# Low parts of the weights on GpSimd in the S5 stage, four small memsets per batch on VectorE, and projection units shared out anew

## The chip, the cores and the metric

One core of a Trainium2 chip runs the whole block in one launch. The metric is the device time of that launch in microseconds (us), as the median of several runs; lower is better. In the profile the engines are PE (TensorE matmuls), PEld (its weight loads), DVE (VectorE), ACT (ScalarE), POOL (GpSimd) and SP (SyncE, which here issues nearly all DMAs). Each engine works through its own list in order, and so does each DMA queue.

## The reference

A decoder block on x (1024 tokens x 1024 channels, float32). The input is normalised and projected by one wide matrix; the pieces of the projection feed an mLSTM branch, an S5 branch and two gates:

```python
xn = rmsnorm(h, norm_pre_g[l])
proj = xn @ w_in[l]
u_a, z_a, o_a, i_a, f_a, u_b, z_b, g_pre = jnp.split(proj, split_points, axis=-1)
y_a = mlstm_branch(...) @ w_a_out[l]
y_b = s5_branch(u_b, z_b, ...) @ w_b_out[l]
g = jax.nn.sigmoid(g_pre)
merged = g[..., :D_MODEL] * y_a + g[..., D_MODEL:] * y_b
h = h + rmsnorm(merged @ w_o[l], norm_post_g[l])
```

The S5 branch is a diagonal complex recurrence over the sequence with 32 groups of 64 states, then a gelu, a product with `w_glu` under a sigmoid (the gate product) and silu(z_b).

## The kernel before, in words

**Matmuls in three passes.** Every large product is made in a rounded 32-bit type. An operand `a` is split in a high part (`a` rounded, made on ACT) and a low part (`a` minus the high part), and a product is three matmuls: high by high, high by low, low by high. For the activations these are the tiles `xh` and `xl`, for the weights `wh` and `wl`. `split_w` (L130) makes a weight's two halves of 128x1024: ACT copies `wh` from the raw tile `wr` (L140), and the subtraction for `wl` (L142) runs on DVE, except for a few later weights whose second half goes to POOL. `wr`, `wh` and `wl` have two buffers each.

**How weights flow.** A planned list (`plan`) fixes the order of the weights. `take` hands out the weight that is due and at once splits the next one (`pump`). After a split, `fetch` asks for the weight after that: an SP DMA of `wr`, which has to wait until ACT and the engine of `wl` have read the old `wr`. SP works in order, so stores that are queued behind this DMA wait with it.

**Units.** The projections for the gates (`g`, seven weights with four units each, after an eighth that is done at the start) and for `z_b` (`zb`, two weights with four units each) are cut in units of 24 matmuls on 512 columns. They lie in a first-in first-out list, `fillers`, and are called units 0 to 35 here: 0 to 27 are `g`, 28 to 35 are `zb`. `take` of a new weight comes with units 0, 4, 8, and so on. `fill(n)` runs the next n. A unit writes one of three PSUM banks (`pp`); ACT makes a tanh of it into one of three `tg` buffers, for `zb` units DVE also multiplies with the bank (L309), and SP stores `tg` to DRAM (`t_d`, `zb_d`).

**The S5 stage.** Its 32 groups are worked in four batches b of eight. Per batch:

- `s5_pre` and `s5_phase` (DVE): tables `w_r`, `w_i`, `v_r`, `v_n`, and the phases `ec_r`, `ec_i` and decays `rho`, in 12 and 42 products and sums and a copy.
- `s5_w`, `s5_k` (PE): transposes of the tables and a small kernel; ACT copies them out, POOL clears `m0` (L647), DVE adds to `kt_` (L644), and DMAs fill `m0` by way of DRAM.
- `s5_x` (PE, 32 small matmuls, L661), and then its chain on DVE: four products with PSUM, two sums, two scans (L675, L676), four products and four sums that end in `ss_`.
- `s5_y` (PE, L701 with `m0` and L702 with `ss_`), gelu on ACT (L705), eight stores to `yg_d`.

POOL sets single columns of `ec_r`, `ec_i`, `rho` and `ss_` by small memsets (L604, L605, L615, L678).

The order around them is written out by hand. Ten units lie ahead of the batches. In each batch stand `s5_w`, `s5_k`, two units, `s5_x`, then on DVE `s5_pre` and `s5_phase` of the next batch, three units (two in the last batch), `s5_y`, one unit. One unit follows the batches. Then the four `yg` tiles are loaded (L738), split into `ygh` (ACT, L742) and `ygl` (DVE, L743), two units follow, and with all 36 used up the gate product (`glu_unit`, on `ygh`, `ygl`) begins.

Of the kernel before, what the change touches and what calls it, by code (L numbers as in the profile page):

```python
# [36 lines left out]
def hybrid_block(ctx, tc, x, norm_pre_g, w_in, conv_w, conv_b, w_q, w_k, w_v, b_i, b_f, head_g,  # L37
# [4 lines left out]
    V, A, PE, PL, SY = nc.vector, nc.scalar, nc.tensor, nc.gpsimd, nc.sync  # L42
# [11 lines left out]
    def mbank():  # L54
        return ps.tile([P, 512], F32, tag="pm", bufs=5, name="pm")
# [54 lines left out]
    def dma_w(parts, kt, ncol):  # L110
# [16 lines left out]
            raws.append((k0, n, raw, 0, ncol))  # L127
        return raws

    def split_w(kt, ncol, raws, between=None, pl=False):  # L130
        wh = wp.tile([P, kt, ncol], F32R, tag="wh", name="wh")
        wl = wp.tile([P, kt, ncol], F32R, tag="wl", name="wl")
        if "M" in cur and kt == 2 and ncol == 512:
            pm = cur.pop("M")
            A.activation(wh[:, :, 0:256], pm, AF.Copy)
            tt(wl[:, :, 0:256], pm, wh[:, :, 0:256].bitcast(F32), ALU.subtract)
            raws = [(0, 2, raws[1], 256, 256)]
        for i, (k0, n, raw, c0, w) in enumerate(raws):
            hi = wh[:, k0:k0 + n, c0:c0 + w]
            A.activation(hi, raw, AF.Copy)  # L140
            eng = PL if (between or pl) and i else V
            eng.tensor_tensor(wl[:, k0:k0 + n, c0:c0 + w], raw, hi.bitcast(F32), op=ALU.subtract)  # L142
            if between and i == 0:
                between()
        return wh, wl
# [14 lines left out]
    def pump(between=None, pl=False):  # L160
        if not ready:
            fetch()
            if raw_q:
                key, kt, ncol, raws = raw_q.popleft()
                ready.append((key, split_w(kt, ncol, raws, between, pl)))
        pending.append(fetch)
# [35 lines left out]
    def run(u):  # L202
        tick()
        pre, body = u
        if pre:
            pre()
        for i in range(min(look[0], len(fillers))):
            if fillers[i][0]:
                fillers[i][0]()
                fillers[i] = (None,) + fillers[i][1:]  # L210
        while early:
            early.pop(0)()
        new = len(stage2)
        body()
        fresh = stage2[new:]
        del stage2[new:]
        step2()
        stage2.extend(fresh)

    def fill(n=1):  # L220
        for _ in range(n):
            if fillers:
                run(fillers.popleft())

    def unit(body, pre=None):
        return (pre, body)
# [137 lines left out]
    def b4k(name, shape, bufs=1, tag=None):  # L364
        return sp.tile(list(shape), F32, tag=tag or name, bufs=bufs, name=name)

    def ub_unit(b, hf):
        if b % 2 == 0 and hf == 0:
            cur["ub"] = take(("ub", b // 2))
        if hf == 0:  # L370
            uc[b] = b4k("uc", (P, TS, P), 4, "u0")
        o = bank()
        proj_cm(o, cur["ub"], (b % 2) * P, xh, xl, HS[hf])
        A.copy(uc[b][:, :, 64 * hf:64 * hf + 64], o.rearrange("p (c t) -> p t c", t=TS))
        if hf:
            ut[b] = b4k("ut", (P, 8, P), 4)
            store(u_d[b], uc[b].rearrange("p t c -> p (t c)"))
            defer(lambda: store(ut[b], u_d[b].rearrange("(g m) (j c) -> (m j) g c", m=NG, j=TS)))
# [12 lines left out]
    def ubstep():  # L391
        if ub_steps:
            b, hf = ub_steps.popleft()
            run(unit(lambda: ub_unit(b, hf)))
        else:
            fill()
# [21 lines left out]
                             src[0, 16 * gh:16 * gh + 16].rearrange("(a b) n p -> b a n p", b=2)[b])  # L418
    for _ in range(4):
        ubstep()  # L420
    pt = mbank()
    for j in range(3):
        PE.transpose(pt[:, j * GP:(j + 1) * GP], prm[:, j, :], ident[:GP, :GP])
# [14 lines left out]
    def tt(o, a, b, op):  # L438
        V.tensor_tensor(o, a, b, op=op)  # L439

    def mul(o, a, b):
        tt(o, a, b, ALU.mult)
# [71 lines left out]
    def cmul(o_r, o_i, xr, xi, yr, yi, t=None, t2=None):  # L514
        n = 1
        for s in o_r.shape[1:]:
            n *= s
        if t is None:
            t = cm_t[0][:, :n]
            if len(o_r.shape) == 3:  # L520
                t = t.rearrange("p (a b) -> p a b", a=o_r.shape[1])
        mul(o_r, xr, yr)
        mul(t, xi, yi)
        tt(o_r, o_r, t, ALU.subtract)
        t2 = t if t2 is None else t2
        mul(o_i, xr, yi)
        mul(t2, xi, yr)
        tt(o_i, o_i, t2, ALU.add)

    def bc(a, shape):  # L530
        return a.to_broadcast(shape)
# [68 lines left out]
    def s5_phase(b):  # L600
        gs = slice(4 * b, 4 * b + 4)

        ec_r, ec_i = b4k("ec_r", (P, 4, P)), b4k("ec_i", (P, 4, P))
        PL.memset(ec_r[:, :, 0:1], 1.0)  # L604
        PL.memset(ec_i[:, :, 0:1], 0.0)  # L605
        te = b4k("te", (P, 4, 64))
        for k in range(7):
            n = 1 << k
            yr = bc(ph[3 + k][0][:, gs].unsqueeze(2), [P, 4, n])
            yi = bc(ph[3 + k][1][:, gs].unsqueeze(2), [P, 4, n])  # L610
            cmul(ec_r[:, :, n:2 * n], ec_i[:, :, n:2 * n], ec_r[:, :, 0:n], ec_i[:, :, 0:n], yr, yi,
                 te[:, :, :n])
        rho = b4k("rho", (P, 4, P))
        V.tensor_copy(rho, bc(rho8[:, gs].unsqueeze(2), [P, 4, P]))
        PL.memset(rho[:, :, 0:1], 0.0)  # L615
        st[b].update(ec=(ec_r, ec_i), rho=rho)

    def s5_w(b):
        q = st[b]
        wt = b4k("wt", (P, 2, 4, P))  # L620
        for ri, w in enumerate(q["w"]):
            pt = mbank()
            for g in range(4):
                PE.transpose(pt[:, g * P:(g + 1) * P], w[:, g].rearrange("p m s -> p (m s)"), ident)
            A.copy(wt[:, ri].rearrange("p g c -> p (g c)"), pt)
        q["wt"] = wt
# [28 lines left out]
    def s5_x(b):  # L655
        q = st[b]
        xr, xi = mbank(), mbank()
        for g in range(4):
            for b2 in range(2):
                for ri, o in enumerate((xr, xi)):  # L660
                    PE.matmul(o[NS * b2:NS * (b2 + 1), g * P:(g + 1) * P],  # L661
                              q["wt"][:, ri, g, NS * b2:NS * (b2 + 1)], ut[b][:, 2 * g + b2, :],
                              start=True, stop=True)
        ec_r, ec_i = q["ec"]
        er, ei = ec_r.rearrange(fl), ec_i.rearrange(fl)
        zr, zi, zt = b4k("zr", (P, 512)), b4k("zi", (P, 512)), b4k("zt", (P, 512))
        zt2 = b4k("zt2", (P, 512))
        mul(zr, xr, er)
        mul(zt, xi, ei)
        mul(zi, xi, er)  # L670
        mul(zt2, xr, ei)
        tt(zr, zr, zt, ALU.add)
        tt(zi, zi, zt2, ALU.subtract)
        rf = q["rho"].rearrange(fl)
        V.tensor_tensor_scan(zr, rf, zr, 0.0, op0=ALU.mult, op1=ALU.add)  # L675
        V.tensor_tensor_scan(zi, rf, zi, 0.0, op0=ALU.mult, op1=ALU.add)  # L676
        ss_ = b4k("ss_", (P, 2, 4, P))
        PL.memset(ss_[:, :, :, 0:1], 0.0)  # L678
        g4 = lambda a: a.rearrange("p (g c) -> p g c", c=P)[:, :, 0:P - 1]
        zrs, zis, t_a, t_b = g4(zr), g4(zi), g4(zt), g4(zt2)  # L680
        ers, eis = ec_r[:, :, 0:P - 1], ec_i[:, :, 0:P - 1]
        mul(t_a, zis, eis)
        mul(t_b, zis, ers)
        mul(zis, zrs, eis)
        mul(zrs, zrs, ers)
        for b2 in range(2):
            rows = slice(NS * b2, NS * (b2 + 1))
            tt(ss_[0:NS, b2, :, 1:], zrs[rows], t_a[rows], ALU.subtract)
            tt(ss_[NS:P, b2, :, 1:], zis[rows], t_b[rows], ALU.add)
        q["s"] = ss_  # L690
# [22 lines left out]
    while ub_steps:  # L713
        ubstep()
    fill(3)
    s5_phase(0)
    for b in range(4):
        s5_w(b)
        s5_k(b)
        fill(2)  # L720
        s5_x(b)
        if b < 3:
            s5_pre(b + 1)
            s5_phase(b + 1)
        fill(3 if b < 3 else 2)
        s5_y(b)
        fill(1)
    s5.close()
# [23 lines left out]
    def load_aux(key, src):  # L752
        t = gq.tile([P, 512], F32, tag="aux", bufs=6, name="aux")
        SY.dma_start(t, src)
        aux[key] = t
# [31 lines left out]
    for i in range(2):  # L787
        for hf in range(2):
            for m in range(4):
                ct = 4 * i + m  # L790
                fillers.append(unit(lambda i=i, m=m, hf=hf: yb_unit(i, m, hf),
                                    lambda ct=ct, hf=hf: load_aux((1, ct, hf), t2_d[ct * P:(ct + 1) * P, HS[hf]])))
    look[0] = 3
    while fillers:
        fill()
    look[0] = 1
# [660 lines left out]
```

## Time and profile before

| what | value |
|---|---|
| median of 3 runs | 1003.8 us (1002.75 to 1004.91) |
| the profiled execution: its own time, its span | 1006.37 us, 1004.3 us |
| PE busy | 976.7 us, 97% of the span |
| DVE, ACT, POOL busy | 61%, 35%, 15% of the span |
| share of PE in the chain that ended last | 83% |
| mean granted TensorE clock | 0.993 |
| S5 batches in the trace | about 146 to 306 us from the start |
| gate product starts | 328.4 us |

A line of the profile gives the kernel's line, engine, operation and the tiles written and read; behind the bar stand busy time, mean duration in ns, and idle time with what ended it. A line of the timeline gives the start in us from the span's start and the duration. In the view of waits the three numbers are the total in us, how often, and the longest.

### The profile page before, as it was taken

How to read it: one execution, taken by the hardware profiler on the slowest of the kernel's cores; microseconds unless marked ns; L12 is line 12 of the kernel's file. 1: busy time of each engine (PE TensorE's matmuls, PEld its weight loads, DVE VectorE, ACT ScalarE, POOL GpSimd, SP SyncE). 2: the span in 40 equal slices, each digit the busy share in tenths (PEclk: the TensorE clock that was granted, in tenths of full speed). 3: DMA queues.
4: the chain of work that ended last, by engine and by line, in shares of the span. 5: the costliest groups of instructions: out<-in, count | busy, mean ns of one | idle time of the engine just before them, and what ended most of it. 6: DMA issues, size and time to landing. Idle time of an engine off the chain costs nothing.

```text
span 1004.3 us, 15220 instructions
## 1 busy us (share of the span) xinstructions
PE 976.7 (97%) x5617; PEld 840.9 (84%) x5617; DVE 615.5 (61%) x1400; ACT 351.1 (35%) x696; POOL 154.6 (15%) x210
## 2 busy tenths in 40 slices
PE   7999999999999999999999999999999999999997
PEld 6888888788778788978988899889987888779997
DVE  4426496686952854254677477747774888675226
ACT  7322131233032531223544355435543452223311
POOL 4001000000000000012112232223221311343001
PEclk8999999999999999999999999999999999999999
DMA  7344221333056447314433354336436796783504
GB/s 253 94 153 157 90 95 36 93 111 109 17 177 187 170 156 253 107 42 126 138 121 131 95 174 131 135 86 184 132 121 215 248 318 202 271 301 118 189 1 168
DMA packets 115449, 148.31 MB, mean 148 GB/s; under 512 B 19080, under 2 KB 71472, under 8 KB 115376
## 3 DMA queue, kind: packets, MB, share of 16 engines
q1 hardware_dynamic: 115376, 147.35, 45.7%
q8 instruction: 44, 0.72, 0.3%
q14 instruction: 29, 0.24, 0.1%
HBM read 100.88 MB, written 46.43 MB: 147 GB/s over the span
## 4 chain that ended last, share of the span: by engine, by line
PE 83%; DVE 10%; DMA 3%; issue 2%; ACT 1%; SPq 0%; POOL 0%; DVEq 0%; POOLq 0%; ACTq 0%
PE pp L180 22%; PE pp L182 22%; PE pp L181 22%; PE pm L182 4%; PE pm L180 4%; PE pm L181 3%; DVE wl L142 1%; PE pm L1084 1%; DMA wr<-in_w_in_dram 1%; DVE zt L439 1%; PE pm L1007 1%; DMA xt<-in_x_dram 1%; DMA ft<-t_d 1%; PE pm L661 1%; DVE ec_r L439 1%
## 5 line engine op out<-in xcount | busy, mean ns | idle before, releaser
L180 PE MATMUL pp<-xh,wh 128*128 128x512 f32 x768 | 307.6, 401 | 3.2 <-DVE xl L276 2.4
L182 PE MATMUL pp<-xh,wl 128*128 128x512 f32 x768 | 305.0, 397 | 4.4 <-DVE wl L142 4.4
L181 PE MATMUL pp<-xl,wh 128*128 128x512 f32 x768 | 304.7, 397 | 0.0
L182 PEld LDWEIGHTS pp<-xh,wl 128*128 128x128 f32 x768 | 145.0, 189 | 41.0 <-DVE wl L142 6.2
L180 PEld LDWEIGHTS pp<-xh,wh 128*128 128x128 f32 x768 | 145.0, 189 | 39.3 <-DVE xl L276 2.7
L181 PEld LDWEIGHTS pp<-xl,wh 128*128 128x128 f32 x768 | 145.1, 189 | 32.7
L142 DVE TENSOR_TENSOR wl<-wr,wh 128x1024 fp32r<-128x1024 f32 (+2 forms) x71 | 83.4, 1211 | 46.3 <-ACT wh L140 41.7
L140 ACT ACTIVATE wh<-wr 128x1024 fp32r<-128x1024 f32 (+2 forms) x76 | 73.2, 1008 | 40.8 <-PE pm L181 30.7
L182 PE MATMUL pp<-wh,ml 128*128 128x256 f32 x256 | 72.8, 284 | 0.5 <-POOL ml L1363 0.5
L180 PE MATMUL pp<-wh,mh 128*128 128x256 f32 x256 | 72.9, 285 | 0.0
L180 PE MATMUL pp<-wh,xh 128*128 128x256 f32 (+1 forms) x256 | 72.0, 281 | 0.0
L181 PE MATMUL pp<-wl,mh 128*128 128x256 f32 x256 | 71.9, 281 | 0.0
L288 ACT ACTIVATE tg<-pp 128x512 f32<-128x512 f32 x32 | 19.1, 599 | 151.1 <-PE pp L182 75.2
L181 PE MATMUL pp<-wl,xh 128*128 128x256 f32 (+1 forms) x256 | 71.8, 280 | 0.0
L182 PE MATMUL pp<-wh,xl 128*128 128x256 f32 (+1 forms) x256 | 71.8, 280 | 0.0
L182 PEld LDWEIGHTS pp<-wh,ml 128*128 128x128 f32 x256 | 48.1, 188 | 0.7 <-POOL ml L1363 0.7
L181 PEld LDWEIGHTS pp<-wl,mh 128*128 128x128 f32 x256 | 48.6, 190 | 0.1
L180 PEld LDWEIGHTS pp<-wh,mh 128*128 128x128 f32 x256 | 48.4, 189 | 0.2 <-ACT mh L1362 0.2
L181 PEld LDWEIGHTS pp<-wl,xh 128*128 128x128 f32 x256 | 48.2, 188 | 0.2
L180 PEld LDWEIGHTS pp<-wh,xh 128*128 128x128 f32 x256 | 48.1, 188 | 0.2
L182 PEld LDWEIGHTS pp<-wh,xl 128*128 128x128 f32 x256 | 48.0, 187 | 0.0
L981 POOL TENSOR_TENSOR hll<-t2k,hlh 128x512 fp32r<-128x512 f32 x16 | 20.8, 1297 | 166.2 <-ACT hlh L980 89.4
(395 smaller groups left out, 1731.5 us busy)
## 6 DMA issues: line engine op xcount, KB each, us to landing
wr<-in_w_in_dram SPq DMA_DIRECT2D x48, 512.0 KB
t_d<-tg SPq DMA_DIRECT2D x32, 256.0 KB
xt<-in_x_dram SPq DMA_DIRECT2D x8, 512.0 KB
aux<-t_d SPq DMA_DIRECT2D x16, 256.0 KB
gb_d<-aux SPq DMA_DIRECT2D x16, 256.0 KB
so_d<-sow SPq DMA_DIRECT2D x32, 128.0 KB
sz_d<-t2k SPq DMA_DIRECT2D x16, 256.0 KB
cs_d<-t2k SPq DMA_DIRECT2D x16, 256.0 KB
```

The costliest lines, as they stand in the source:

```text
L140: A.activation(hi, raw, AF.Copy)
L142: eng.tensor_tensor(wl[:, k0:k0 + n, c0:c0 + w], raw, hi.bitcast(F32), op=ALU.subtract)
L180: PE.matmul(o, lh, rh, start=first, stop=False)
L181: PE.matmul(o, lh, rl, start=False, stop=False)
L182: PE.matmul(o, ll, rh, start=False, stop=last)
L288: A.activation(t, o, AF.Tanh, scale=0.5)
L439: V.tensor_tensor(o, a, b, op=op)
L661: PE.matmul(o[NS * b2:NS * (b2 + 1), g * P:(g + 1) * P], q["wt"][:, ri, g, NS * b2:NS * (b2 + 1)], ut[b][:, 2 * g + b2, :], start=True, st ...
L981: PL.tensor_tensor(lo, acc, hi.bitcast(F32), op=ALU.subtract)
L1007: PE.matmul(pm[:, 256 * k:256 * k + 256], wt[:, e, 256 + P * k:256 + P * k + P], wt[:, e, 0:256], start=e == 0, stop=e == 1)
L1084: PE.matmul(sc[:, :P], k_[:, m, sl], q_[:, m, sl], start=m == 0, stop=m == 1)
```

## The change

The flag `lo_pool` is set after the fourth of the eight `ub` units (the projections that feed S5) and taken back when the gate product's units are started. While it is set, `split_w` gives both low halves of a weight to POOL. This holds for ten weights: the seven `g` of the units, the two `zb` and the gate product's own.

```diff
+    lo_pool = [False]
...
-            eng = PL if (between or pl) and i else V
+            eng = PL if lo_pool[0] or (between or pl) and i else V
...
     for _ in range(4):
         ubstep()
+    lo_pool[0] = True
...
-        PL.memset(ec_r[:, :, 0:1], 1.0)
-        PL.memset(ec_i[:, :, 0:1], 0.0)
+        V.memset(ec_r[:, :, 0:1], 1.0)
+        V.memset(ec_i[:, :, 0:1], 0.0)
...
-        PL.memset(rho[:, :, 0:1], 0.0)
+        V.memset(rho[:, :, 0:1], 0.0)
...
-        PL.memset(ss_[:, :, :, 0:1], 0.0)
+        V.memset(ss_[:, :, :, 0:1], 0.0)
...
     for b in range(4):
         s5_w(b)
         s5_k(b)
-        fill(2)
+        fill(1 if b < 3 else 2)
         s5_x(b)
         if b < 3:
             s5_pre(b + 1)
             s5_phase(b + 1)
-        fill(3 if b < 3 else 2)
+        fill(3)
         s5_y(b)
         fill(1)
...
     look[0] = 3
+    lo_pool[0] = False
     while fillers:
         fill()
```

The units keep their order. The first three batches have five units each now and the last has six, so units 10 to 30 lie in the batches (10 to 32 before), and six units, 30 to 35, stand between the last `s5_y` and the gate product, where four stood.

What moves on POOL: the rows from the clearing of the `bd` tables (ahead of the batches) to the causal masks of the next stage. Before:

```order
L550 MEMSET bd_i 128x512
L604 MEMSET ec_r 128x4
L605 MEMSET ec_i 128x4
L615 MEMSET rho 128x4
L647 MEMSET m_1435 128x1024
L678 MEMSET ss__1532 128x8
```

And now, in the same place and on through all four batches:

```order
L553 MEMSET bd_i 128x512
L144 TENSOR_TENSOR wl<-wr,wh 128x1024 x4
L650 MEMSET m_1435 128x1024
L144 TENSOR_TENSOR wl<-wr,wh 128x1024 x2
L650 MEMSET m_1763 128x1024
L144 TENSOR_TENSOR wl<-wr,wh 128x1024 x2
L650 MEMSET m_2091 128x1024
L144 TENSOR_TENSOR wl<-wr,wh 128x1024 x4
L650 MEMSET m_2425 128x1024
L144 TENSOR_TENSOR wl<-wr,wh 128x1024 x4
L819 MEMSET tri 128x128
```

The small memsets are gone from POOL, and between two clearings of `m0` (`m_...`) stand two to four halves of low parts.

On DVE, the end of the last batch's tables and the start of its chain behind `s5_x`. Before:

```order
L614 COPY rho<-rex 128x512
L142 TENSOR_TENSOR wl<-wr,wh 128x1024 x2
L644 SCALAR_TENSOR_TENSOR kt__2505<-eye_1213,par,kt__2505 128x16
L142 TENSOR_TENSOR wl<-wr,wh 128x1024 x2
L309 SCALAR_TENSOR_TENSOR tg<-tg,pp 128x512 x2
L439 TENSOR_TENSOR zr<-pm,ec_r 128x512
```

And now:

```order
L617 COPY rho<-rex 128x512
L618 MEMSET rho 128x4
L647 SCALAR_TENSOR_TENSOR kt__2417<-eye_1213,par,kt__2417 128x16
L442 TENSOR_TENSOR zr<-pm,ec_r 128x512
L442 TENSOR_TENSOR zt<-pm,ec_i 128x512
```

Four halves of low parts and the products of two `zb` units have left the place ahead of `zr`, the first product of the chain.

On ACT, from the last gelu to the gate product's first tanh (`par` is its bias). Before:

```order
L705 ACTIVATE yg<-pm 128x4x128 x2
L140 ACTIVATE wh<-wr 128x1024 x2
L308 ACTIVATE tg<-pp 128x512 x2
L742 ACTIVATE ygh_2794<-yg_2792 128x1024
L742 ACTIVATE ygh_2800<-yg_2798 128x1024
L742 ACTIVATE ygh_2806<-yg_2804 128x1024
L742 ACTIVATE ygh_2812<-yg_2810 128x1024
L308 ACTIVATE tg<-pp 128x512 x2
L140 ACTIVATE wh<-wr 128x1024 x2
L764 ACTIVATE tg<-pp,par 128x512
```

And now:

```order
L708 ACTIVATE yg<-pm 128x4x128 x2
L310 ACTIVATE tg<-pp 128x512 x2
L745 ACTIVATE ygh_2726<-yg_2724 128x1024
L745 ACTIVATE ygh_2732<-yg_2730 128x1024
L745 ACTIVATE ygh_2738<-yg_2736 128x1024
L745 ACTIVATE ygh_2744<-yg_2742 128x1024
L142 ACTIVATE wh<-wr 128x1024 x2
L310 ACTIVATE tg<-pp 128x512 x4
L142 ACTIVATE wh<-wr 128x1024 x2
L767 ACTIVATE tg<-pp,par 128x512
```

Four tanh instead of two now follow the four `ygh`, and the split of the gate product's own weight has moved from ahead of them to behind them.

## The prediction

> **What bounds the kernel now.** First the page's busy times, then PE's waits in the stretch from 60 to 340 us, which holds all that the change touches.
>
> ```profile
> PE 976.7 (97%) x5617; PEld 840.9 (84%) x5617; DVE 615.5 (61%) x1400; ACT 351.1 (35%) x696; POOL 154.6 (15%) x210
> ```
>
> ```profile
> PE pp L182 <- DVE wl L142: 2.2, 2, 1.1
> PE pm L702 <- DVE ss__2622 L439: 2.0, 2, 1.3
> PE pp L181 <- DVE ygl L743: 1.9, 2, 1.0
> ```
>
> PE is the bound, and the change leaves its matmuls as they are. It can only win back time that PE loses, and in this stretch PE loses it in three places, each waiting for DVE: twice for the low part of a weight, twice for `ss_` in the last `s5_y`, twice for `ygl` at the gate product. What each place costs is read better from PE's timeline, from start to start of equal work, because it also holds slow matmuls.
>
> ```profile
> 187.40 0.27 PE L624 MATMUL pm<-ident,w_r 128*128 128x128 f32 x1
> ...
> 201.70 2.02 PE L661 MATMUL pm<-ut,wt 128*64 128x128 f32 x32
> ...
> 220.55 0.38 PE L701 MATMUL pm<-ut,m 128*128 128x128 f32 x2
> ...
> 224.04 0.48 PE L180 MATMUL pp<-xh,wh 128*128 128x512 f32 x1
> ...
> 229.74 0.38 PE L624 MATMUL pm<-ident,w_r 128*128 128x128 f32 x2
> ...
> 242.69 2.02 PE L661 MATMUL pm<-ut,wt 128*64 128x128 f32 x32
> ...
> 298.29 0.38 PE L701 MATMUL pm<-ut,m 128*128 128x128 f32 x2
> 299.99 0.46 PE L702 MATMUL pm<-ss__2622,vs 128*128 128x128 f32 x2 [1.31 <-DVE ss__2622 L439]
> ...
> 301.40 0.72 PE L702 MATMUL pm<-ss__2622,vs 128*128 128x128 f32 x2 [0.73 <-DVE ss__2622 L439]
> ...
> 305.92 0.48 PE L180 MATMUL pp<-xh,wh 128*128 128x512 f32 x1
> ...
> 328.41 0.40 PE L180 MATMUL pp<-ygh,wh 128*128 128x512 f32 x1
> ...
> 333.88 0.50 PE L180 MATMUL pp<-ygh,wh 128*128 128x512 f32 x1
> ...
> 336.77 0.39 PE L180 MATMUL pp<-ygh,wh 128*128 128x512 f32 x1
> ```
>
> - From `s5_w` to `s5_x` the batch at 229.74 takes 12.95 us, the batch at 187.40, with a wait for `wl`, 14.30: 1.35 lost. The other wait for `wl` is as long, so 2.7 in all.
> - `s5_y` takes 224.04 - 220.55 = 3.49, the last one 305.92 - 298.29 = 7.63: 4.1 lost. Only 2.0 of this is waiting.
> - The gate product's first two units of 12 matmuls take 5.47 and 2.89: 2.6 lost.
>
> Together 9.4 us. The 2.1 in the last `s5_y` that aren't waiting are clock:
>
> ```profile
> 300.00:306.00 6.00, 5.27 (x31) 5.11 (x31) 2.52 (x4) 0.24 (x1) 0.00 (x0) 0.72 0.24 90
> ```
>
> The granted clock is 0.72 over 6 us, so 1.7 us are lost by a slow clock right behind two gaps of 1.31 and 0.73. I take it that it goes with the gaps. [...]
>
> **The change part by part.**
>
> *Low parts off DVE.* Why DVE is late, from its timeline around a batch, the queues' waits and the groups:
>
> ```profile
> 161.38 0.69 DVE L439 TENSOR_TENSOR zr<-pm,ec_r 128x512 f32<-128x512 f32 x1 [9.30 <-PE pm L661]
> ...
> 172.94 0.69 DVE L439 TENSOR_TENSOR w_r<-bb_r,pv_r 128x512 f32<-128x512 f32 x1
> ...
> 181.07 0.16 DVE L439 TENSOR_TENSOR ec_r<-ec_r,ph_r 128x4 f32<-128x4 f32 x1
> ...
> 189.50 2.35 DVE L142 TENSOR_TENSOR wl<-wr,wh 128x1024 fp32r<-128x1024 f32 x2
> ...
> 289.74 0.68 DVE L439 TENSOR_TENSOR zr<-pm,ec_r 128x512 f32<-128x512 f32 x1
> ```
>
> ```profile
> SPq L124 <- DVE wl L142: 86.3, 10, 30.0
> ```
>
> ```profile
> ACT tg L288 <- DMA t_d<-tg: 36.4, 3, 16.0
> ```
>
> The chain behind `s5_x` takes 172.94 - 161.38 = 11.6 us, `s5_pre` 8.1, `s5_phase` 8.4: 28.1 per batch. A low part is queued behind all of it. Its `wr` stays taken, so SP stands up to 30 us in front of the next load, the stores of `tg` stand behind SP, and ACT waits up to 16 us for a `tg` buffer. On POOL the low part starts when `wh` is there, some 20 us before its first matmul, so both waits for `wl` go: -2.7. In the last batch the chain starts at 289.74 instead of the end of `s5_x` at 285.04 + 2.02, held by two halves and two `zb` products: 2.7 late. Both are gone now.
>
> What POOL pays, and DVE with it:
>
> ```profile
> L142 DVE TENSOR_TENSOR wl<-wr,wh 128x1024 fp32r<-128x1024 f32 x62 | 76.3, 1267 | 46.3 <-ACT wh L140 41.7 <-PE pm L182 4.5
> ...
> L142 POOL TENSOR_TENSOR wl<-wr,wh 128x1024 fp32r<-128x1024 f32 x4 | 9.9, 2475 | 12.2 <-ACT wh L140 12.2
> ```
>
> ```profile
> 874.52 1.29 POOL L1363 TENSOR_TENSOR ml<-ft,mh 128x512 fp32r<-128x512 f32 x1
> ```
>
> ```profile
> 895.43 3.42 POOL L1363 TENSOR_TENSOR ml<-ft,mh 128x512 fp32r<-128x512 f32 x2 [5.37 <-ACT mh L1362]
> ```
>
> ```profile
> 895.32 0.69 DVE L439 TENSOR_TENSOR ft<-ft,fpa 128x512 f32<-128x512 f32 x1
> 895.93 0.68 DVE L1358 SCALAR_TENSOR_TENSOR ft<-ft,pp 128x512 f32<-128x512 f32 x1
> 896.65 1.07 DVE L439 TENSOR_TENSOR ft<-ft,fpa 128x512 f32<-128x512 f32 x1
> ```
>
> A half costs 2.48 us on POOL against 1.27 on DVE. And the two engines shut each other out: the sum of two SBUF tiles takes DVE 0.69 alone and 1.07 while POOL runs, and POOL 1.71 instead of 1.29 while DVE does; a product with PSUM (0.68) goes through. [...] This speaks against the change: DVE would lose up to 2 x 2.48 = 5.0 us per weight where it saved 2.5. I charge the full 5.0 wherever a split meets DVE's SBUF work. The rows allow from 0 (the split falls where DVE is idle or reads PSUM) to 5.0 per weight.
>
> *Units shared out anew.* A unit is 229.74 - 224.04 = 5.7 us, and from `s5_x` to `s5_y` with three units 18.85 (220.55 - 201.70), of which `s5_x` itself is 2.0. In the first and last batch a split starts behind the first of these units, and lands in the second half of the chain: 11.6 + 5.0 = 16.6 us, with the memset of `ss_` 16.7 (a DVE memset of so few elements is bounded by 0 and the 0.16 of the smallest sum above; I take 0.1). `s5_y` comes 16.9 us behind `s5_x`, and needs the first `ss_` 0.2 later. So the last `s5_y`, with a unit more in front of it, no longer waits: -4.1. The slack is only 0.4. In the second batch the split falls on the products with PSUM (one half free, 2.5 left), in the third, the split is made before `s5_x`: no wait there.
>
> The whole batch: five units make PE's period 12.95 - 5.7 + 18.85 + 3.49 + 5.7 = 35.3 us, against 41.0 before. DVE has 28.1 + 0.5 for five memsets + 5.0 = 33.6. It keeps up, with 1.7 to spare. On POOL the clearing of `m0` now queues behind the splits; the nearest one is that of unit 24, just ahead of the last batch, whose 5.0 us are over before unit 25 ends, and the loads of `m0` are issued only behind that unit: 0.
>
> *Behind the batches.* `ygl` was late because four units, 22.5 us (328.41 - 305.92), cover the way of `yg` through DRAM. Six units cover it now: -2.6. But the loads are queued on SP behind the store of the second unit's `tg`, and ACT has a new order:
>
> ```profile
> 318.04 0.69 DVE L309 SCALAR_TENSOR_TENSOR tg<-tg,pp 128x512 f32<-128x512 f32 x1 [4.91 <-ACT tg L308]
> ```
>
> ```profile
> 319.19 1.83 SPq L738 DMA_DIRECT2D yg<-yg_d  x4
> ```
>
> ```profile
> 325.27 5.94 ACT L742 ACTIVATE ygh<-yg 128x1024 fp32r<-128x1024 f32 x3 [0.29 <-DMA yg<-yg_d]
> 331.11 1.07 ACT L308 ACTIVATE tg<-pp 128x512 f32<-128x512 f32 x2
> 332.06 2.00 ACT L140 ACTIVATE wh<-wr 128x1024 fp32r<-128x1024 f32 x2
> ```
>
> From the issue of the loads to the last `ygh` it is 331.2 - 319.19 = 12.0 us. Then `wh` of the gate product (2.0), the tanh of unit 32 (0.6) and its product on DVE (0.7) have to be over before unit 35 may write the same bank: 15.3 us. A unit is 22.5 / 4 = 5.62 there, so the second one ended at 305.92 + 11.24 = 317.2, and the issue came 2.0 behind it. Now, 2.0 + 15.3 = 17.3 us after the second unit (31) the bank is free, and unit 35 is due three units after it, at 16.9. A new wait of 0.4. The gate product's `wl` on POOL is ready some 5 us after its `wh`, still before its first matmul: 0. Behind that, `w_b_out` is loaded later, but is wanted eight units later: 0.
>
> *Sum.* -2.7 - 4.1 - 2.6 + 0.4 = -9.0 us. The profiled execution took 1006.37 for a span of 1004.3, so it would take 997.4. The median of the runs is 2.6 below it; the same gain there gives 1003.8 - 9.0 = 994.8.
>
> **The rivals.**
>
> 1. *`s5_y` waits again.* The slack of 0.4 is smaller than one DVE sum. If the chain is 1 us late in one or two batches and the clock falls once behind it (1.7), 2 to 4 come back: 997 to 999. For it: POOL's stretch from 1.29 to 1.71. [...]
> 2. *The gate product's handover costs more*, by a slower way of `yg` or by SP, which now stands before `w_b_out` until POOL has read `wr`. 1 to 4 us: 996 to 999.
> 3. *The slow clock isn't the gaps' doing*, and stays: 1.7 less, 996.5.
> 4. *No change:* another wait stands right behind (`tg` buffers, `wr`) and PE's gaps move on instead of closing: about 1003.
> 5. *Slower: DVE becomes the bound of the batches.* Should one half on POOL hold DVE for over 4 us instead of 2.5 (its own time and then waiting in turn), 28.6 + 1.25 weights x 8 = 38.6 per batch pass PE's 35.3. It decides at 2.7 us per half. Each batch then loses 3.3 and a slow clock of 1.7, 15 us in three batches, against 9.0 gained: about 1010.
>
> **How the numbers follow.** The forecast has 0.55 (994 to 996), rival 1 0.18, rival 2 0.13, rival 3 0.05, rival 4 0.04, rival 5 0.05. The range goes from 993.0, where all 9.4 us come back and the runs scatter by 1 us (1002.75 to 1004.91 before), to 999.0, the upper end of rivals 1 and 2. A measurement of this kernel can tell 0.2%, 2 us, from no change. Faster by over 0.2%: 0.91; within it: 0.04; slower: 0.05.
>
> **What would show it.** Right: PE's waits for `wl`, `ss_` and `ygl` are gone between 60 and 340 us; the clock is 1.00 throughout; the gate product starts at about 328.4 - 2.7 - 4.1 + 0.4 = 322.0; `s5_x` follows `s5_x` by 35.3; SP's wait for `wl` (86.3) is mostly gone; DVE's sums are stretched where POOL runs. Wrong: PE waits for `ss_` in several batches, or a second stretch of low clock, or DVE without a gap from batch to batch.

## The result, and the profile after

The changed kernel takes 994.43 us (median of 5 runs, 993.79 to 998.49) against 1002.75 for the kernel before on the same chip (1001.88 to 1004.91). The ratio is 0.9916, with a 95% interval of 0.9894 to 0.9938. On another chip, later, it was 0.9912 (0.9887 to 0.9938).

First the page of the changed kernel, its engines' busy times. Its lines are two to four further down: the three passes are L182 to L184, the split is L142 and L144.

```profile
span 992.7 us, 15204 instructions
...
PE 971.8 (98%) x5617; PEld 836.6 (84%) x5617; DVE 625.5 (63%) x1396; ACT 351.8 (35%) x696; POOL 203.1 (20%) x214
```

POOL has 48.5 us more to do, and PE is busy for 4.9 us less although it runs the same 5617 matmuls: the slow ones are gone (the mean granted clock is 0.999, 0.993 before). PE's waits over the whole span begin so:

```profile
PE pp L182 <- DVE xl L278: 2.5, 1, 2.5
PE pp L184 <- DVE wl L144: 2.2, 2, 1.3
```

The first is the start of the kernel, the second the end of attention (about 857 us). From 60 to 340 us the view of waits has no row for PE: those for `wl`, `ss_` and `ygl` are all gone. The busy times by batch, from `s5_w` to `s5_w` (the last row to the unit behind `s5_y`), first before, then after; the last columns are the granted clock, the share of the DMA engines and GB/s:

```profile
146.40:187.40 41.00, 41.00 (x234) 33.58 (x233) 30.66 (x89) 11.49 (x18) 1.17 (x5) 1.00 0.13 43
187.40:229.74 42.34, 41.26 (x234) 33.50 (x233) 29.85 (x67) 11.83 (x19) 1.25 (x5) 1.00 0.41 121
229.74:270.73 40.99, 40.99 (x234) 33.58 (x232) 32.03 (x85) 10.21 (x17) 1.25 (x5) 1.00 0.26 73
270.73:305.92 35.19, 32.06 (x185) 26.20 (x184) 20.70 (x31) 8.42 (x15) 1.11 (x3) 0.95 0.47 146
```

```profile
144.02:179.46 35.44, 35.44 (x209) 29.06 (x208) 25.69 (x48) 10.89 (x17) 6.35 (x3) 1.00 0.34 92
179.46:214.85 35.39, 35.39 (x210) 29.07 (x208) 31.81 (x91) 9.61 (x16) 5.73 (x3) 1.00 0.32 93
214.85:250.25 35.40, 35.40 (x209) 29.05 (x208) 29.97 (x70) 11.50 (x18) 8.46 (x4) 1.00 0.34 93
250.25:285.56 35.31, 35.31 (x210) 29.05 (x208) 23.57 (x44) 9.29 (x16) 7.31 (x4) 1.00 0.39 116
```

In each row stand the length, then PE, PEld, DVE, ACT and POOL. PE's second number now equals the length in every batch, at a clock of 1.00, and a batch with five units takes 35.4. DVE has up to 31.8 of it, so it keeps up.

The two ends of the stretch, in PE's timeline:

```profile
144.02 0.60 PE L627 MATMUL pm<-ident,w_r 128*128 128x128 f32 x4
...
319.55 0.40 PE L182 MATMUL pp<-ygh,wh 128*128 128x512 f32 x1
```

From the first `s5_w` to the gate product it is 175.5 us now, 328.41 - 146.40 = 182.0 before: 6.5 won. The first two units of the gate product win 2.9 more (5.5 instead of 8.4), 9.4 in all. The profiled executions differ by 11.9 (1006.37 and 994.43), since the first `s5_w` itself comes 2.4 earlier after, which no edit makes (the part on the clock at the end says what does). The medians differ by 8.3. A second profile of the changed kernel has 175.2 us for the same stretch, so 0.3 is no difference here.

### The profile page after: what moved, and what is told of

The parts are those of the page before. It is cut to its first block, busy times and chain, and to the rows that moved or that the text cites. A ratio compares the mean times of both kernels' runs of the same rounds, so it can differ in the third digit from the quotient of the medians.

```text
span 992.7 us, 15204 instructions
## 1 busy us (share of the span) xinstructions
PE 971.8 (98%) x5617; PEld 836.6 (84%) x5617; DVE 625.5 (63%) x1396; ACT 351.8 (35%) x696; POOL 203.1 (20%) x214
## 4 chain that ended last, share of the span: by engine, by line
PE 85%; DVE 4%; DMA 4%; issue 3%; ACT 2%; POOL 1%; SPq 1%; DVEq 0%; POOLq 0%; ACTq 0%
PE pp L182 23%; PE pp L184 23%; PE pp L183 23%; PE pm L184 4%; PE pm L182 3%; PE pm L183 3%; DVE wl L144 1%; DMA wr<-in_w_in_dram 1%; PE pm L1088 1%; PE pm L664 1%; PE pm L705 1%; PE pm L704 1%; PE pm L1011 1%; DMA xt<-in_x_dram 1%; DMA ft<-t_d 1%
## 5 line engine op out<-in xcount | busy, mean ns | idle before, releaser
L182 PE MATMUL pp<-xh,wh 128*128 128x512 f32 x768 | 306.3, 399 | 3.3 <-DVE xl L278 2.5
L184 PE MATMUL pp<-xh,wl 128*128 128x512 f32 x768 | 303.6, 395 | 2.2 <-DVE wl L144 2.2
L182 PEld LDWEIGHTS pp<-xh,wh 128*128 128x128 f32 x768 | 144.1, 188 | 39.9 <-DVE xl L278 2.8
L184 PEld LDWEIGHTS pp<-xh,wl 128*128 128x128 f32 x768 | 144.1, 188 | 37.9 <-DVE wl L144 3.1
L144 POOL TENSOR_TENSOR wl<-wr,wh 128x1024 fp32r<-128x1024 f32 (+1 forms) x25 | 61.6, 2481 | 227.3 <-ACT wh L142 227.3
L142 ACT ACTIVATE wh<-wr 128x1024 fp32r<-128x1024 f32 (+2 forms) x76 | 73.2, 1009 | 41.5 <-PE pm L183 30.6
L144 DVE TENSOR_TENSOR wl<-wr,wh 128x1024 fp32r<-128x1024 f32 (+2 forms) x51 | 59.9, 1207 | 21.7 <-ACT wh L142 17.2
L184 PE MATMUL pp<-wh,ml 128*128 128x256 f32 x256 | 72.2, 282 | 0.5 <-POOL ml L1367 0.5
L182 PE MATMUL pp<-wh,mh 128*128 128x256 f32 x256 | 72.1, 282 | 0.0
L182 PE MATMUL pp<-wh,xh 128*128 128x256 f32 (+1 forms) x256 | 72.0, 281 | 0.0
L184 PE MATMUL pp<-wh,xl 128*128 128x256 f32 (+1 forms) x256 | 71.8, 280 | 0.0
L184 PEld LDWEIGHTS pp<-wh,ml 128*128 128x128 f32 x256 | 48.2, 188 | 0.7 <-POOL ml L1367 0.7
L182 PEld LDWEIGHTS pp<-wh,mh 128*128 128x128 f32 x256 | 48.2, 188 | 0.3 <-ACT mh L1366 0.2
L182 PEld LDWEIGHTS pp<-wh,xh 128*128 128x128 f32 x256 | 48.0, 188 | 0.2
```

The costliest lines, as they stand in the source:

```text
L182: PE.matmul(o, lh, rh, start=first, stop=False)
L184: PE.matmul(o, ll, rh, start=False, stop=last)
```

## The experiments

The change has three edits. Five kernels leave out one or two of them, or a part of one; the memsets alone, with the old sharing and the low parts on DVE, were not run. In the table each has its median, the ratio of its runs to those of the kernel before on its chip, and the time from the first `s5_w` to the gate product in its trace.

| kernel | low parts on POOL | memsets on DVE | new sharing | median us | ratio (95%) | stretch us |
|---|---|---|---|---|---|---|
| before | no | no | no | 1002.75 | 1 | 182.0 |
| units only | no | no | yes | 1006.11 | 1.0008 (0.9996 to 1.002) | 185.3 |
| low parts back on DVE | no | yes | yes | 1006.55 | 1.0011 (0.9993 to 1.003) | 184.1 |
| low parts only | yes | no | no | 1007.92 | 1.0028 (1.0012 to 1.0044) | 184.6 |
| memset of `rho` back on POOL | yes | four of five | yes | 1004.42 | 0.9989 (0.9971 to 1.0007) | 182.5 |
| old sharing | yes | yes | no | 998.83 | 0.9931 (0.9912 to 0.995) | 175.2 |
| changed | yes | yes | yes | 994.43 | 0.9916 (0.9894 to 0.9938) | 175.5 |

**Units only.**

```diff
-        fill(2)
+        fill(1 if b < 3 else 2)
...
-        fill(3 if b < 3 else 2)
+        fill(3)
```

> Before, with only the new sharing of units; low parts stay on DVE, the small memsets on GpSimd. My theory: the three losses are separate. The last s5_y (4.1) and the gate product (2.6, less 0.4) are won by the units alone. The two waits of 1.35 for wl go, but one of 2 to 3.3 us comes at unit 20: its low part is queued on DVE behind the chain of the second batch, s5_pre and s5_phase (28.1 us behind s5_x, then 2.5 of its own), and with a unit less ahead of s5_x the unit is due about 30 us behind it. So 1002.75 - 6.3 = 996.5, up to 997.5. Rival 'the units do it all': no wait for wl is left, 994.4 as in the changed kernel. Rival 'DVE sets the batches': waits for wl and for tg's buffers in several batches, 999 or more.

Measured: no gain at all, 1.0008. The last `s5_y` no longer waits, as all expected, but the third batch loses more than that wins. Its timelines there, in the order of what hangs on what (DVE, SP's queue, ACT, PE):

```profile
218.06 2.35 DVE L142 TENSOR_TENSOR wl<-wr,wh 128x1024 fp32r<-128x1024 f32 x2
...
219.31 1.52 SPq L124 DMA_DIRECT2D wr<-in_w_in_dram  x2
220.93 1.44 SPq L82 DMA_DIRECT2D t_d<-tg  x3
...
227.39 0.60 ACT L288 ACTIVATE tg<-pp 128x512 f32<-128x512 f32 x1 [16.19 <-DMA t_d<-tg]
227.88 1.07 ACT L625 COPY wt<-pm 128x512 f32<-128x512 f32 x2
...
228.52 1.82 PE L661 MATMUL pm<-ut,wt 128*64 128x128 f32 x12 [3.79 <-ACT wt L625]
```

The low part is made at 218.06, at the end of DVE's `s5_phase`. Only then may SP issue the next load of `wr`, and three stores of `tg` stand behind that load. ACT waits 16.2 us for one of those buffers, and the copy of `wt`, which `s5_x` needs, is queued on ACT behind the waiting tanh. So `s5_x` waits 3.79 for something that was ready in PSUM 11 us earlier. In the kernel before ACT waited as long (16.0), and with two units ahead of `s5_x` PE did not feel it. I had counted only PE's own wait for `wl` (1.06 here) and missed ACT's queue; and the gap is followed by 6.8 us at half clock, another 3.0 in that batch. Behind the batches PE waits 1.6 more for DVE's product of a `zb` unit.

**Low parts only.** The changed kernel's flag `lo_pool`, with the sharing and the memsets of before. "The lock" is in the expectations the author's name for what a half on POOL costs DVE beside it: in the changed kernel's last chain two operations of 0.68 us each take 2.77 there.

> The changed kernel's low parts on GpSimd, with the old sharing of units and the memsets on GpSimd. My theory: the waits for wl go (2.7), and with DVE free the last chain starts at the end of s5_x instead of 2.7 late, so that the two units there (11.3 us) cover it up to the first ss_ (the chain of 11.6 less its last two sums): the 4.1 of the last s5_y go too, slow clock included. The wait for ygl (2.6) stays. 1002.75 - 2.7 - 4.1 = 996.0. Rival 'the last s5_y needs the third unit': it still waits about 1 to 2 us and draws a slow stretch, 998 to 1000. Rival 'the lock takes it back': s5_y waits in earlier batches, 1000 or more.

Measured: slower than before, 1.0028. Of the three theories only the last one's number fits (1000 or more); its mechanism, a wait of `s5_y` in earlier batches, does not. PE's longest waits from 40 to 340 us:

```profile
PE pp L184 <- POOL wl L144: 5.0, 2, 2.5
PE pp L183 <- DVE ygl L746: 1.9, 2, 0.9
PE pm L704 <- issue: 1.5, 1, 1.5
```

The waits for `wl` are not gone, they have grown from 2.2 to 5.0. POOL's own waits and its timeline say why:

```profile
POOL rho L618 <- DVE rho L617: 66.6, 4, 19.4
```

```profile
188.19 0.10 POOL L618 MEMSET rho<- 128x4 f32 x1 [19.35 <-DVE rho L617]
188.33 4.67 POOL L144 TENSOR_TENSOR wl<-wr,wh 128x1024 fp32r<-128x1024 f32 x2
```

A memset of 0.10 us stands in POOL's list ahead of the low part, and waits 19.35 us for the copy of `rho`, the last instruction of DVE's `s5_phase`. The low part has left DVE's queue and still comes behind all of DVE's work, and then takes 4.7 instead of 2.4. The memsets of `ec_r` and `ec_i` stand in the same list and wait too (18.68 just before this); whether they alone would be enough was not run. The row for `rho` was there in the profile of before, where no wait of PE hung on it, since POOL had no low part to make in these batches:

```profile
POOL rho L615 <- DVE rho L614: 107.7, 4, 49.6
```

**One memset back.** The test of this: the changed kernel with only the memset of `rho` on POOL.

```diff
-        V.memset(rho[:, :, 0:1], 0.0)
+        PL.memset(rho[:, :, 0:1], 0.0)
```

> The changed kernel with one of the five memsets per batch, that of rho's first column (0.1 us), back on GpSimd. New theory, from the run with the low parts alone: this memset waits for DVE's s5_phase, and every low part behind it on GpSimd waits with it (there GpSimd waited 66.6 us for rho in four places). So the low parts come 28 us behind s5_x again, the load queue stands, tg's stores stand behind it, ScalarE waits for tg's buffer with wt queued behind it, and s5_x waits. As with the units alone, where that cost 5.2 and 3.0 us in the second and third batch, and 1.2 to 2.4 more since a half takes 2.4 instead of 1.2: 9 to 12 us over the changed kernel, about the time of before or 2 above it. The theory of the prediction, in which a memset is 0.1 us of work: no difference, 8.5 below before.

Measured: 1004.42, ratio 0.9989 where the changed kernel has 0.9916. One instruction of 0.1 us on another engine takes back 7.3 us of the 8.4; the stretch is 7.0 longer. POOL's timeline in the second batch, with the memset back, and then of the changed kernel:

```profile
218.14 0.10 POOL L618 MEMSET rho<- 128x4 f32 x1 [29.61 <-DVE rho L617]
218.28 4.67 POOL L144 TENSOR_TENSOR wl<-wr,wh 128x1024 fp32r<-128x1024 f32 x2
```

```profile
188.74 4.77 POOL L144 TENSOR_TENSOR wl<-wr,wh 128x1024 fp32r<-128x1024 f32 x2 [13.88 <-ACT wh L142]
```

The same weight is split at 188.74 when nothing stands ahead of it, and at 218.28 behind the memset. The theory of the prediction, a memset as 0.1 us of work, falls. The new one gave the mechanism, and somewhat too high a price (9 to 12).

**Low parts back on DVE**, with the new sharing and all memsets on DVE (the line `lo_pool[0] = True` taken out).

> The changed kernel with the low parts back on DVE: new sharing and memsets on VectorE alone. New theory: what blocks is DVE's queue itself, a low part stands behind the chain, s5_pre and s5_phase wherever the memsets are. So as with the units alone: waits of about 1 for wl and 4 for wt in the third batch and two grid cells of slow clock behind them, within 2 us of before. Rival 'the memsets carry the gain, the low parts don't matter': 5 or more below before.

Measured: 1.0011, as with the new sharing alone (1.0008). The stretch is 184.1, and among PE's waits are

```profile
PE pm L663 <- ACT wt L627: 3.5, 1, 3.5
PE pp L184 <- DVE wl L144: 1.4, 1, 1.4
```

So under the new sharing neither edit brings a gain without the other: the low parts have to leave DVE's queue, and the memsets that wait for DVE have to leave POOL's.

**Old sharing.** The changed kernel without the third edit.

```diff
-        fill(1 if b < 3 else 2)
+        fill(2)
...
-        fill(3)
+        fill(3 if b < 3 else 2)
```

> The changed kernel with the old sharing of units: low parts on GpSimd and memsets on VectorE alone. If the low parts and the memsets together carry the gain: no wait for wl (2.7 won), the last s5_y no longer waits although two units stand before it (its chain starts at the end of s5_x, 11.6 us, the first pair of ss_ 1.4 earlier, and it is read 11.4 behind the chain's start: 4.1 won), the wait for ygl (2.6) stays. 6.8 below before; s5_x follows s5_x by 41.0. Rival 'the new sharing is needed too': waits for wl or ss_ stay, as in both single runs, within 2 of before. Rival 'the lock': the split falls into the last chain, a gap and a slow stretch there, 3 to 5 below before.

Measured: 998.83, ratio 0.9931, which is 6.9 below before (6.8 expected). PE's only row of waits from 40 to 365 us:

```profile
PE pp L183 <- DVE ygl L746: 1.8, 2, 1.0
```

The last `s5_y` does not wait although only two units stand before it: in this order no split falls into its chain, which takes 283.10 to 294.62 = 11.5 us, and the first pair of `ss_` is there at 293.20, before `s5_y` at 294.33. The stretch, 175.2, is as long as with the new sharing (175.5 and 175.2 in its two profiles). What the sharing wins is the wait for `ygl`: from the start of the gate product to the last matmul it is 669.1 us here, 666.5 and 666.7 in the changed kernel. By the times alone this part, 1.5 us, is not settled, since the two intervals overlap.

**Two units before the last `s5_y`** in the changed kernel, with the third behind it.

```diff
-        fill(3)
+        fill(3 if b < 3 else 2)
```

> The changed kernel with two units instead of three between s5_x and s5_y in the last batch (the third comes behind it). My theory: with the split on GpSimd, its chain takes 15.7 us from the start of its first product to its end, two units and the rest give 11.4 before the first ss_ is read (17.06 less 5.64). The first pair of ss_ is ready 1.4 before the chain's end: a wait of 2.9, and 0.7 to 1.4 more for the second; if the split falls behind the chain instead (one unit fewer runs ahead of the first half) the wait shrinks. A stretch of slow clock of 1.7 lost behind it. 994.4 + 3.6 + 1.7 = 999.7. Rival 'the lock costs the chain nothing that s5_y sees': no wait, 994.4. Rival 'the slow clock does not follow gaps': the wait without the slow stretch, 998.

Measured: 1001.06, ratio 0.9967 against 0.9916, 5.1 over the changed kernel (5.3 expected). Its `s5_y` takes 10.0 us (276.25 to 286.30):

```profile
279.31 0.49 PE L705 MATMUL pm<-ss__2526,vs 128*128 128x128 f32 x2 [2.68 <-DVE ss__2526 L442]
...
280.73 0.80 PE L705 MATMUL pm<-ss__2526,vs 128*128 128x128 f32 x2 [0.66 <-DVE ss__2526 L442]
```

Of the 6.6 lost, 3.3 are gaps and the rest is slow clock, 6.8 us of it at one half. Set beside the old sharing, where two units suffice: the new sharing moves a split into the last chain, and the third unit covers what that costs. What the split costs DVE can be read in its timeline of the changed kernel, where POOL starts on it at 272.88:

```profile
273.24 2.77 DVE L442 TENSOR_TENSOR zr<-zr,ec_r 128x508 f32<-128x508 f32 x1
276.04 2.77 DVE L442 TENSOR_TENSOR ss__2526<-zr,zt 64x508 f32<-64x508 f32 x1
278.82 0.68 DVE L442 TENSOR_TENSOR ss__2526<-zi,zt 64x508 f32<-64x508 f32 x1
```

Two operations of 0.68 take 2.77, about as long as the half on POOL beside each (2.58 and 2.85): 4.2 per split, not the 5.0 that was charged.

**A longer chain.** Does a gap of PE bring the slow clock? Six, and then four, more products of 0.69 us in the last chain of the changed kernel write the same numbers again.

```diff
         mul(t_a, zis, eis)
+        if b == 3:
+            for _ in range(6):
+                mul(t_a, zis, eis)
```

> The changed kernel with six more DVE products of 0.69 us (the same product written again, results unchanged) in the chain of the last batch: 4.1 us longer. In the profile of the changed kernel the first pair of ss_ is ready 2.8 us before it is read, the second 1.8 before. So two gaps of about 1.3 and 1.0 us in the last s5_y, as in the kernel before (1.31 and 0.73). If gaps of this size bring the slow clock: granted 0.7 over some 3 to 6 us behind them, 1.7 more, 994.4 + 2.3 + 1.7 = 998.4. If the slow clock there had another cause: clock 1.00 behind them, 996.7. If the slack is larger than the trace says: 994.4.

> The changed kernel with four more DVE products of 0.69 us in the last chain instead of six: 2.8 us longer, against 2.8 and 1.8 us to spare for the first and second pair of ss_. So no gap before the first read, or one under 0.1, and one of about 1.0 before the second. From the traces so far, slow stretches start on a grid of 3.413 us and follow a cell in which PE was busy for no more than half (0.49 and less; 0.51 and more had none). A gap of 1.0 leaves 0.7 of a cell busy, so no slow stretch: 1.0 over the changed kernel, where six products cost 4.1. Rival 'any wait in s5_y brings it': 2.7 to 3 over.

Measured with six: ratio 0.9958, 4.2 over the changed kernel, and `s5_y` takes 7.63 us, to the hundredth what it took before the change. The gaps, and the clock from 282.50 on in steps of 3.41 us:

```profile
284.79 0.49 PE L708 MATMUL pm<-ss__2526,vs 128*128 128x128 f32 x2 [1.44 <-DVE ss__2526 L442]
...
286.20 0.79 PE L708 MATMUL pm<-ss__2526,vs 128*128 128x128 f32 x2 [0.70 <-DVE ss__2526 L442]
```

```profile
282.50:285.91 3.41, 1.56 (x9) 1.08 (x7) 3.28 (x6) 0.60 (x1) 0.00 (x0) 1.00 0.01 2
285.91:289.32 3.41, 3.12 (x14) 3.12 (x15) 1.52 (x3) 0.00 (x0) 0.00 (x0) 0.50 0.40 154
289.32:292.74 3.42, 3.42 (x23) 3.05 (x22) 0.00 (x0) 1.08 (x2) 0.00 (x0) 1.00 0.06 10
```

The clock is 0.50 for exactly one step and full again. With four products, `s5_y` waits once, for 0.7 us, and takes 4.72 instead of 3.49; no slow stretch follows (its pairs of 128x128 matmuls take 0.39 us behind the gap, 0.63 in the slow stretch with six). The kernel takes 996.9 beside the changed kernel's 995.62, 1.3 over it (1.0 expected), though here the intervals of the ratios overlap. Gaps of 2.1 together brought the slow clock, one of 0.7 did not.

**Low parts made twice**, which doubles POOL's work on them while the flag is set.

```diff
             eng.tensor_tensor(wl[:, k0:k0 + n, c0:c0 + w], raw, hi.bitcast(F32), op=ALU.subtract)
+            if lo_pool[0]:
+                eng.tensor_tensor(wl[:, k0:k0 + n, c0:c0 + w], raw, hi.bitcast(F32), op=ALU.subtract)
```

> The changed kernel with each low part on GpSimd made twice (the second writes the same numbers). In the changed kernel a split that meets the chain lengthens it by 4.2 us (15.7 against 11.5) in the first and last batch and by 2.1 in the second, and s5_y has 1.8 to spare. Made twice, the lock takes up to 5 more: gaps of about 2.5 to 3 us in the first and the last s5_y and a slow stretch of 2.0 behind each: 9 to 10 over the changed kernel, about as before. Rival 'DVE becomes the bound' (the prediction's fifth): each batch has 38 us of DVE for 35.4 of PE, waits in all batches and slow stretches: 15 over the changed kernel, slower than before. Rival 'the lock hits what would have been idle': within 2 of the changed kernel.

Measured: 1023.65, ratio 1.0186 (1.0161 to 1.021), 27 over the changed kernel. The rival won, and was itself too low. Busy times by batch:

```profile
145.16:190.05 44.89, 38.35 (x209) 30.86 (x208) 42.01 (x88) 10.97 (x17) 14.11 (x7) 0.92 0.35 90
190.05:226.16 36.11, 35.63 (x209) 29.16 (x208) 34.30 (x77) 9.62 (x16) 12.30 (x5) 1.00 0.34 90
226.16:263.46 37.30, 36.11 (x209) 29.16 (x208) 36.46 (x70) 11.50 (x18) 13.68 (x6) 1.00 0.31 88
263.46:310.05 46.59, 37.68 (x210) 30.46 (x208) 37.27 (x69) 9.37 (x16) 19.00 (x8) 0.93 0.29 85
```

DVE is busy for 150.0 of the 164.9 us (111.0 of 141.5 in the changed kernel): it is now the bound. A piece of its timeline, with the second of the four halves that POOL makes meanwhile:

```profile
260.16 2.84 DVE L444 TENSOR_TENSOR v_r<-v_r,tv 128x576 f32<-128x576 f32 x1
262.46 2.76 POOL L146 TENSOR_TENSOR wl<-wr,wh 128x1024 fp32r<-128x1024 f32 x1
262.93 2.92 DVE L444 TENSOR_TENSOR v_n<-crn,pw_i 128x576 f32<-128x576 f32 x1
265.76 2.89 DVE L444 TENSOR_TENSOR tv<-ct_t,pw_r 128x576 f32<-128x576 f32 x1
268.69 2.78 DVE L444 TENSOR_TENSOR v_n<-v_n,tv 128x576 f32<-128x576 f32 x1
```

Four operations of 0.75 take 11.4 us, 8.4 more than alone. POOL's halves start at 259.73, 262.46, 265.19 and 268.12: in these rows the two engines go in turn, one instruction each. The loss is not spread evenly. Most of it comes where a late table holds `s5_k`: PE's gaps for `ec_i` and `v_r` are 11.0 us (6.7 the longest). Waits for `ss_` in all four batches add 6.2, and two stretches of 6.8 and one of 3.4 us run at the slow clock.

**The last split.** PE's remaining wait for `wl` at 857 us, taken away by giving one split more to POOL.

```diff
+    lo_pool[0] = True
     cur["ya"] = take(("ya", 3))
+    lo_pool[0] = False
```

> The changed kernel with one split more on GpSimd, that of the last slice of the w_a output weights at the end of attention. In the changed kernel PE waits 2.2 us in two places there (0.98 and 1.26) for a low part that DVE makes late (its halves take 2.3 instead of 1.2 beside GpSimd). On GpSimd, which is free then, it should be ready before: 2.2 less than the changed kernel, 10.6 below before. Rivals: the low part takes 2.4 a half there too and is as late: same as the changed kernel; DVE's other work there stands longer under the lock and PE waits for it: slower than the changed kernel by up to 2.

> The changed kernel itself once more, as the measure for the two beside it: 8.3 below before (ratio 0.9916), no wait of PE between 60 and 340 us. Its two waits of 0.98 and 1.26 for wl at about 857 us stand again, and where they fall into one cell of the grid a slow stretch of 3.4 follows (1.7 us): then it takes 2 more.

> The kernel with the last split on GpSimd once more, beside the changed kernel on the same chip. If the 2.2 us of waiting for wl at the end of attention are won, and with them the chance of a slow stretch behind (1.7): 2 to 3 below the changed kernel. If the gain of the first run of it was the scatter between chips: within 1.

Measured: 994.09 with ratio 0.9887 (0.9866 to 0.9907) in the first run. Beside the changed kernel on one chip it is 994.75 against 995.62, ratios 0.9900 and 0.9912 with intervals that overlap. What is shown is the wait: 2.2 us become 0.3. (In the second run of the changed kernel the two waits, 0.99 and 1.27, stand again, and no slow stretch follows: the matmuls of 128x512 behind them take 0.39 to 0.50 us.)

```profile
PE pp L184 <- POOL wl L144: 0.3, 1, 0.3
```

In the second trace 0.7 of it comes back at about 890 us, where PE waits for `ft` as it does not in the changed kernel. From the gate product to the last matmul the two traces take 665.3 and 666.4, the changed kernel's 666.5 and 666.7. So it is 0.1 to 1.4 us faster in the traces, and by the times alone that is not settled.

## Why the prediction was right

The time (994.8, measured 994.43) and all three terms came out, but two of the reasons did not hold. That the time is met to 0.4 us is in part luck: the gain was put at 9.0 and measured at 8.3, and the median of before, 1003.8 in its first three runs, is 1002.75 over five.

- **`wl`, 2.7: right, for a reason left out.** "On POOL the low part starts when `wh` is there" is true only because the memsets left POOL. The step that failed is "a DVE memset of so few elements is bounded by 0 and the 0.16 of the smallest sum": it priced them as work on the engine they go to, not as waits on the engine they leave. With one of them back, 7.3 of the 8.4 us are gone. That the term came out all the same is luck too: the change happened to move the memsets, and the prediction gave no reason why it had to.
- **The last `s5_y`, 4.1: right in size.** It was to be won by the chain's earlier start "with a unit more in front of it". The earlier start alone does it (old sharing). The extra unit is needed only since the new sharing puts a split into that chain.
- **Its slack, 0.4: too small.** It set the end of the chain against the first reading of `ss_`, but the first pair of `ss_` is ready 1.4 before that end (279.50 and 280.92 in the changed kernel). The chain took 15.7 instead of 16.7, and the first pair was there 2.8, the second 1.8, ahead of its reading. Four extra products (2.8 us) cost one gap of 0.7, which fits this slack.
- **What POOL costs DVE, 5.0 in full: near.** That DVE stands for the whole of both halves, 2 x 2.48, was the author's estimate, and no run shows the 5.0. DVE lost 4.2 in the first and the last batch, 2.1 in the second (predicted 2.5), nothing in the third (predicted 0). In the changed kernel an operation on two SBUF tiles takes 2.77 where POOL's halves take 2.58 and 2.85; in its second batch the four products with PSUM, beside a half of 2.41, keep their 0.68 to 0.69.
- **`ygl`, 2.6: right.** The sharing alone carries it: behind the start of the gate product, the traces with the old and the new sharing differ by 2.6 and 2.4. The new wait of unit 35, forecast at 0.4, is 0.2: it starts at 313.84 behind a matmul that started at 313.41, where 0.23 is the step without a wait.
- **`s5_x` to `s5_x` by 35.3: measured 35.4.** The gate product was to start at 322.0 and started at 319.55. With the 2.4 added by which the first `s5_w` was early, that is 321.9.
- **SP's wait for `wl` "mostly gone": wrong.** From 60 to 340 us it is 53.0, where it was 92.6, in shorter pieces (the longest 14.4, 30.0 before). What is gone is ACT's wait for the stores to `t_d`, 36.4 before; one wait of 8.4 for a store to `zb_d` has come, and PE does not wait behind it:

```profile
SPq L124 <- POOL wl L144: 53.0, 17, 14.4
ACT tg L310 <- DMA zb_d<-tg: 8.4, 1, 8.4
```

- **Rival 1** (`s5_y` waits again) did not come, since its lateness was inside the real slack. **Rival 2** cost 0.2. **Rival 4** was closer than it looked: with one memset left on POOL it is what happens. **Rival 5** did not come, since a half held DVE for about 2.1 in the batches, under its threshold of 2.7. But it is near: made twice, the low parts hold DVE for up to 8.4 us per weight, 4.2 per half, and DVE became the bound.
- **Rival 3** (the slow clock isn't the gaps' doing) falls with the longer chain: behind gaps of 1.44 and 0.70, which the added products made, the clock was 0.50 for 3.41 us.

## What to carry to other kernels

Before work is moved to an idle engine, read what that engine waits for: an idle engine's queue may hold a tiny instruction that waits for the very engine that is to be relieved, and everything behind it waits too (here a memset of 0.10 us waited 19.35, and 4.67 us of low parts stood behind it). Here a queue was freed only when both the moved work and the waiting instructions were sorted out, so test edits together as well as one by one: the low parts without the memsets brought nothing (1.0028), nor did the memsets without the low parts, under the new sharing (1.0011), and together they gave four fifths of the gain (6.9 of 8.4 us). When a stall has been hidden by a unit of other work, moving that unit can uncover it elsewhere, as it did with the new sharing alone, so follow a late buffer through the load queue, the store queue and the next engine's list to its end.

## What the runs showed of the hardware

**When the clock was slow.** In the trace of before the clock has two values, 1.00 and 0.50. Its slow stretches start at 14.73 and 301.45 us, 286.72 apart, and last for 6.827 and 3.413: two steps and one of 3.413, 84 steps apart (the one behind the last matmul aside). With six more products the two that the rows here show start at 285.91 and 862.76, 576.85 apart, 169 of these steps. The "grid" and its "cells" in the expectations are these steps. Read step by step, with PE's busy time by the profile:

| trace | step, us | PE busy in it, us | clock behind it |
|---|---|---|---|
| units only | 224.37 to 227.78 | 0.35 | 0.50 for two steps |
| two units before the last `s5_y` | 276.44 to 279.85 | 0.73 | 0.50 for two steps |
| memset of `rho` back on POOL | 216.63 to 220.04 | 1.34 | 0.50 for two steps |
| low parts only | 186.85 to 190.26 | 1.35 | 0.50 for one step |
| before | 298.04 to 301.45 | 1.36 | 0.50 for one step |
| before | 11.32 to 14.73 | 1.38 | 0.50 for two steps |
| six more products | 282.50 to 285.91 | 1.56 | 0.50 for one step |
| six more products | 859.35 to 862.76 | 1.66 | 0.50 for one step |
| before | 4.49 to 7.91 | 1.66 | 1.00 |
| changed | 10.78 to 14.20 | 1.96 | 1.00 |
| changed | 14.20 to 17.61 | 2.04 | 1.00 |
| changed | 857.28 to 860.69 | 2.15 | 1.00 |
| changed | 853.87 to 857.28 | 2.43 | 1.00 |

In these rows the clock was 0.50 behind steps with 1.66 us of PE or less, with one exception, and 1.00 behind those with 1.96 or more. In the first of two slow steps PE was busy for 2.68 to 2.78 us; a slow step that stood alone had 2.92 to 3.42. So the same two gaps cost nothing in one trace and a slow step in another. The waits for `wl` at the end of attention, 2.2 us together, first in the changed kernel (0.98 and 1.26), then in the one with the longer chain:

```profile
853.87:857.28 3.41, 2.43 (x11) 1.68 (x10) 3.41 (x3) 0.63 (x1) 3.41 (x2) 1.00 0.94 278
857.28:860.69 3.41, 2.15 (x9) 1.45 (x9) 3.38 (x4) 0.00 (x0) 0.58 (x1) 1.00 1.00 372
```

```profile
859.35:862.76 3.41, 1.66 (x6) 0.70 (x5) 3.41 (x2) 0.05 (x1) 2.77 (x2) 1.00 0.98 320
862.76:866.17 3.41, 2.92 (x7) 2.34 (x8) 3.02 (x5) 0.23 (x1) 0.00 (x0) 0.50 1.07 377
```

In the first the gaps fall into two steps, PE is busy for 2.43 and 2.15 of 3.41, and the clock stays at 1.00. In the second one step holds 1.75 us without PE, PE is busy for 1.66, and the next step runs at 0.50.

**This is also scatter between launches.** The start of the kernel, where PE waits for its first data, costs no slow step in the profile after, one in its second profile (15.54 to 18.95) and two in that of before (14.73 to 21.56); the first `s5_w` stands at 144.02, 145.34 and 146.40. The five runs of the changed kernel fit this: their mean clock is 0.999 in the three of 993.79 to 994.43 us, 0.995 in that of 997.04 and 0.994 in that of 998.49, though where the slow steps of the last two lay is not known, since only one of the five has a profile. So stretches are compared from a common event, not from the start.
